# A two-layer encoder trunk with mixture of experts: weights split by whole chunks on ScalarE and VectorE, with none of it on GpSimd

## The chip, the cores and the metric

The kernel runs on one core of a Trainium2 chip. The metric is the device time of one execution in microseconds. Of the kernel before there are three runs: 1071.22 us (median), 1070.33 and 1071.66.

## The reference

The input is a residual stream x of 512 rows of 1024 floats, and 256 memory rows. Two layers follow each other. In each layer

- one projection of x feeds a token mixer (layer 0: a gated unit over chunks of 128 rows; layer 1: a short causal convolution) and the queries of a cross-attention to the memory rows; both results are concatenated, projected, added to 2^0.5 x and normalised;
- a router, shared by the layers, picks for each row one group of four experts and two experts in it; each of the 16 experts computes `silu(x @ w_gate) * (x @ w_up)` and then `@ w_down`, weighted by the router's share; the sum is added to 2^0.5 x and normalised.

```
h = jax.nn.silu(xt @ w_gate[e]) * (xt @ w_up[e])
out = out + combine[:, e:e + 1] * (h @ w_down[e])
```

w_gate and w_up are 1024 x 512 and w_down is 512 x 1024 for each expert, all float32: 6 MB an expert, 96 MB a layer. All results are float32 and are wanted close to float32 precision.

## The kernel before

**Splitting.** TensorE multiplies in the type fp32r, which keeps fewer bits than float32. So each operand is split into a high part (a copy rounded to fp32r, made on ScalarE) and a low part (what the rounding left, float32 minus high, made on VectorE, or for some weights on GpSimd). `mm3` makes a product of three matmuls: high with high, high with low, low with high.

**Pages.** SBUF is handed out in 24 pages of 8 KB a partition. `page` takes the front of a list of free pages, `drop` puts pages at its end. A page taken anew is a new tile in the same memory, and the framework lets an instruction that writes it wait for those that still use the bytes it writes.

**The stream of weights** (class `Stream`, one object `W`). All weights pass through it as chunks of 1 MB, one page each: 128 partitions x 4 x 512 floats. `fetch` takes a page, and SyncE's queue loads a chunk into it; a load also waits for the load two before it. `split` takes a page for one *half* of the oldest chunk (2 x 512 floats a partition) and puts its high part in the front half of that page and its low part in the back half; after the second half of a chunk its raw page is dropped. `next` gives the oldest half that is ready; `done` drops its page and calls `pump`. `pump` splits as long as fewer than `ahead` halves are ready, and else fetches as long as more pages are free than `keep` and what splitting still wants. All this happens while the program is written, so it fixes which page each instruction uses and the order in which the stream's work is issued; the framework's planner then sets the order on each engine from its own estimate of times.

**The experts** (`experts`). Each expert handles up to 128 rows, gathered by an indirect DMA on GpSimd's queue three experts ahead. `gate_up` takes eight halves (gate, up, gate, up, two chunks' worth of rows each), six fp32r matmuls of 512 columns for a half; then Silu on ScalarE (line 651) and the product on VectorE (line 652). `down` of the expert before takes four halves, its results are evicted on ScalarE (line 673) and added to memory by an indirect DMA. For the last expert, `down` of expert 14 stands between its two gate/up halves. That makes twelve halves, six chunks, for each expert, 96 chunks a layer. In the experts `ahead` is 4 and `keep` is 1; after expert 12 (`last - 3`) `keep` becomes 6. Three pages besides those of the stream are in use there. The halves whose running number modulo 12 is 5 or 11 have their low part made on GpSimd, as has one late half of each layer; around the routers every second one (layer 0) or two of three (layer 1).

**The other stages.** The projections use 24 matmuls for each half, with `keep` 2 to 8 and `ahead` 4 (3 or 2 around the routers).

The lines 130 (high part) and 131 (low part) are the split; lines 161 to 163 are the three matmuls of `mm3`.

Of the kernel before, what the change touches and what calls it, by code (L numbers as in the profile page):

```python
# [19 lines left out]
FR = mybir.dt.float32r  # L20
BF = mybir.dt.bfloat16
I32 = mybir.dt.int32
AF = mybir.ActivationFunctionType
# [25 lines left out]
def trunk(ctx, tc, x, mem, w_in_a, sgu_ln_g, sgu_ln_b, sgu_w, sgu_b, w_in_b, conv_w, w_kv, w_out,  # L49
# [15 lines left out]
    def page(name, shape, dtype=FT):  # L65
        assert free_pages, f"no page for {name}; held: {sorted(v[1] for v in held.values())}"
        i = free_pages.pop(0)
        uid[0] += 1
        t = pages.tile(shape, dtype, name=f"{name}_{uid[0]}", tag=f"pg{i}", bufs=1)
        held[id(t)] = (i, name, t)  # L70
        return t

    def drop(*ts):
        for t in ts:
            free_pages.append(held.pop(id(t))[0])
# [8 lines left out]
        return psum.tile([P, n], FT, name=name, tag="R", bufs=1)  # L84


    class Stream:
        def __init__(self):
            self.todo, self.raw, self.ready = [], [], []
            self.keep, self.ahead, self.stop, self.sent = 0, 4, 0, 0  # L90
            self.pooled = ()
            self.hold, self.count, self.on_pool = False, 0, lambda n: False
            self.after, self.behind, self.loads = None, None, []

        def add_pairs(self, w, k0):
# [14 lines left out]
        def fetch(self):  # L110
            self.sent += 1
            t = page("raw", [P, 4, 512])
            src = self.todo.pop(0)
            with ExitStack() if self.behind is None else tc.issue_after(self.behind):
                load = sp.dma_start(t if src.ap[-1][1] == 512 else t.rearrange("p (a b) n -> p a (b n)", a=2), src).ins
            self.loads.append(load)
            if len(self.loads) > IN_FLIGHT:
                tc.add_manual_dep(load, self.loads.pop(0).name,
                                  mybir.DependencyInfo(mybir.DependencyClass.Sync, mybir.DependencyReason.DATA),
                                  reason="few loads in flight")  # L120
            self.raw.append([t, 0])

        def split(self):
            r = self.raw[0]
            t, h = r
            g = page("split", [P, 2, 2, 512], FR)
            src = t[:, 2 * h:2 * h + 2]
            low = pool_e if self.on_pool(self.count) or self.count in self.pooled else vec
            with ExitStack() if self.after is None else tc.issue_after(self.after):
                act.activation(g[:, 0], src, AF.Copy)  # L130
            low.tensor_tensor(g[:, 1], src, g[:, 0], op=OP.subtract)  # L131
            self.count += 1
            self.ready.append(g)
            r[1] += 1
            if r[1] == 2:
                self.raw.pop(0)
                drop(t)

        def pump(self):
            while True:  # L140
                if not self.hold and len(self.ready) < self.ahead and self.raw and len(free_pages) > 0:
                    self.split()
                elif len(self.todo) > self.stop and len(free_pages) > self.keep + max(0, self.ahead - len(self.ready)):
                    self.fetch()
                else:
                    return
# [3 lines left out]
                self.pump()  # L150
            return self.ready.pop(0)

        def done(self, g):
            drop(g)
            self.pump()

    W = Stream()
# [451 lines left out]
    def experts(i, lnp, fill, after, stop, fine=False):  # L609
# [71 lines left out]
        more(i, hy)  # L681
        W.keep = 1
        W.pump()
        W.on_pool = lambda n: n % 12 in (5, 11)
        xtrans(0)
        gather(2)
        for e in range(E):
            if e == last - 1 and not fine:
                rows = page("lnrow", [2 * KB, P])
                for u, v in enumerate(lnp):  # L690
                    act.dma_start(rows[u * KB:(u + 1) * KB], v.rearrange("(k p) -> k p", p=P))
            up = gate_up(e, (lambda: (down(last - 1, scaled(last - 1)), scatter(last - 1))) if e == last else None)
            if e + 1 < E:
                xtrans(e + 1)
            if e + 3 < E:
                gather(e + 3)
            if 0 < e < last:
                down(e - 1, scaled(e - 1))
                scatter(e - 1)
            if e == last - 3:  # L700
                n = W.count + 2 * (len(W.raw) + len(W.todo) - stop) - (W.raw[0][1] if W.raw else 0)
                W.pooled = [n - k for k in (3,)]
                W.keep = 6
                W.stop = stop - 2 if stop else 0
            if e == last:
                drop(xt, xg)
                selp = page("selt", [P, 2, NC, P], FT)
                for c in range(NC):
                    vec.tensor_scalar(selp[:, 0, c, :], slot1, posp[:, c, last:last + 1], None, op0=OP.is_equal)
                t = bank([P, NC, P], "selt")  # L710
                for c in range(NC):
                    pe.transpose(t[:, c, :], selp[:, 0, c, :], ident)
                selt = page("selr", [P, NC, P], FR)
                vec.tensor_copy(selt, t)
                drop(selp)
                xs[:] = [page("x", [P, 2, D]) for _ in range(2)]
                xrow[:] = [xs[c // 2][:, c % 2, :] for c in range(NC)]
                if fine:
                    with tc.issue_after(added[last - 1].ins):
                        lnp = ln_params(*lnp, pool_e)  # L720
                for c in range(NC):
                    W.behind = sp.dma_start(xrow[c], rd[i][c * P:(c + 1) * P, :]).ins
            if e < last:
                htrans(e)
# [3 lines left out]
            act.activation(yp[:, 0, n], o, AF.Copy, scale=tabs[last][1])  # L728
            vec.scalar_tensor_tensor(yp[:, 1, n], o, tabs[last][1], yp[:, 0, n], op0=OP.mult, op1=OP.subtract)
        W.stop = 0  # L730
        W.on_pool = lambda n: False
        rs, mvs, nms = {}, {}, {}
        r = {}

# [270 lines left out]
    def mixer_end(i, ch, cl, lnp):  # L1005
        lg = [tiny(3 * E, "lg"), None]

        def after(c, normed):
            if c == 0:
                W.on_pool = (lambda n: n % 2 == 1) if i == 0 else (lambda n: n % 3 != 0)  # L1010
                W.keep, W.ahead = (2, 3) if i == 0 else (1, 2)
                W.pump()
            if c == NC - 1:
                lg[1] = bank([P, E], "lg3")
                lg.append(normed)
            logits(c, i, lg[1] if c == NC - 1 else lg[0][:, c * E:(c + 1) * E])
            if c % 2:
                drop(xs[c // 2])
            if c == 1:
                W.pump()  # L1020
        project_out(i, ch, cl, lnp, after)
        drop(lnp)
        rp = page("route", [P, 2048])
        route(0, 3, lg[0].rearrange("p (n e) -> p n e", e=E), lg[2], rp)
        route(3, 1, lg[1].rearrange("p (n e) -> p n e", e=E), lg[2], rp)
        tables()
        drop(rp)
        overflow()
        W.ahead = 4
# [91 lines left out]
```

## Time and profile before

| | |
|---|---|
| runs | 1071.22 us median (1070.33 to 1071.66) |
| the profiled execution | 1070.24 us, of which the span from the first to the last instruction is 1068.4 us |
| mean granted TensorE clock | 0.979 |
| busy: TensorE matmul, weight load | 1002.9 us (94%), 807.4 us (76%) |
| busy: VectorE, ScalarE, GpSimd | 796.7 us (75%), 658.4 us (62%), 321.5 us (30%) |
| moved by DMA | 272.30 MB, 255 GB/s in the mean |

Matmuls overlap their neighbours, so the sum of their durations is more than TensorE's busy time, and the distance from start to start is their pace. The experts of layer 0 run from about 210 to 535 us, those of layer 1 from about 730 to 1040 us. In the timelines an instruction's busy time does not include its waiting; the idle time of the engine ahead of it stands in brackets with what ended it.

### The profile page before, as it was taken

Reading aid. Unit: us, or ns where it says so; the run is one execution under the profiler, and the core shown is the slowest. Engines: PE = TensorE matmul, PEld = TensorE weight load, DVE = VectorE, ACT = ScalarE, POOL = GpSimd, SP = SyncE. Lnnn points to the kernel's source line nnn. Section 1 sums busy time; section 2 is a strip of 40 time slices with the busy share of each in tenths; the row PEclk is TensorE's granted clock in tenths of the full one; section 3 lists DMA queues with packets and bytes.
Section 4 is the critical chain, followed back from the end, with each engine's and each line's share of the span. In section 5 each row is a group of like instructions: output and inputs, shape, how many; then the busy total and the mean of one; then the engine's idle time right before and its main releaser. Section 6 shows DMA issues by size and latency. Waiting matters only on the chain.

```text
span 1068.4 us, 13339 instructions
## 1 busy us (share of the span) xinstructions
PE 1002.9 (94%) x4847; PEld 807.4 (76%) x4848; DVE 796.7 (75%) x1004; ACT 658.4 (62%) x876; POOL 321.5 (30%) x178
## 2 busy tenths in 40 slices
PE   8999999699999999899999999977999999999895
PEld 6788889587777777677678887866777777777663
DVE  4648667768888888678694565664888889887875
ACT  4536524377888888578643424234888888887762
POOL 0000014243544435233310000123444435453253
PEclk9999999999999999899999999977999999999998
DMA  9713449689999999999561423585999999999734
GB/s 322 271 40 118 156 163 322 248 287 311 308 312 334 339 325 343 327 331 342 194 235 41 158 79 121 207 336 175 320 308 344 326 341 335 329 340 328 258 61 160
DMA packets 101968, 272.30 MB, mean 255 GB/s; under 512 B 10426, under 2 KB 10966, under 8 KB 101896
## 3 DMA queue, kind: packets, MB, share of 16 engines
q1 hardware_dynamic: 89480, 242.84, 63.7%
q0 software_dynamic: 11520, 25.92, 8.9%
q10 hardware_dynamic: 896, 2.63, 0.8%
q8 instruction: 39, 0.64, 0.2%
q14 instruction: 33, 0.27, 0.1%
HBM read 261.18 MB, written 26.21 MB: 269 GB/s over the span
## 4 chain that ended last, share of the span: by engine, by line
PE 26%; DVE 11%; issue 10%; ACT 6%; DMA 3%; POOL 1%; DVEq 0%; POOLq 0%; SPq 0%; ACTq 0%
DVE split L131 7%; ACT split L130 5%; PE ya L162 2%; PE ya L163 2%; PE za L162 2%; PE za L163 2%; PE za L161 2%; PE ya L161 2%; PE oa L161 1%; PE oa L163 1%; PE oa L162 1%; PE ra L739 1%; DMA raw<-in_w_down_dram 1%; DMA raw<-in_w_gate_dram 1%; DMA rd<-y,idxs 1%
## 5 line engine op out<-in xcount | busy, mean ns | idle before, releaser
L131 DVE TENSOR_TENSOR split<-raw,split 128x1024 fp32r<-128x1024 f32 x370 | 517.0, 1422 | 119.8 <-ACT split L130 117.4
L130 ACT ACTIVATE split<-raw 128x1024 fp32r<-128x1024 f32 x444 | 457.7, 1057 | 164.3 <-DVE split L131 45.8
L131 POOL TENSOR_TENSOR split<-raw,split 128x1024 fp32r<-128x1024 f32 x74 | 181.7, 2455 | 569.9 <-ACT split L130 267.9
L162 PE MATMUL ya<-split,ht 128*128 128x512 f32 x256 | 106.0, 414 | 11.2 <-DVE split L131 11.2
L162 PE MATMUL ua<-split,xgt 128*128 128x512 f32 x256 | 105.0, 410 | 7.7 <-DVE split L131 6.5
L162 PE MATMUL ga<-split,xgt 128*128 128x512 f32 x256 | 103.8, 405 | 1.9 <-DVE split L131 1.7
L161 PE MATMUL ga<-split,xgt 128*128 128x512 f32 x256 | 103.0, 402 | 0.0
L163 PE MATMUL ya<-split,ht 128*128 128x512 f32 x256 | 101.4, 396 | 0.7 <-DVE ht L167 0.7
L161 PE MATMUL ua<-split,xgt 128*128 128x512 f32 x256 | 101.5, 397 | 0.2 <-ACT split L130 0.2
L161 PE MATMUL ya<-split,ht 128*128 128x512 f32 x256 | 101.6, 397 | 0.0
L163 PE MATMUL ua<-split,xgt 128*128 128x512 f32 x256 | 101.1, 395 | 0.0
L163 PE MATMUL ga<-split,xgt 128*128 128x512 f32 x256 | 100.6, 393 | 0.0
L162 PEld LDWEIGHTS ya<-split,ht 128*128 128x128 f32 x256 | 48.4, 189 | 31.5 <-DVE split L131 21.9
L162 PEld LDWEIGHTS ua<-split,xgt 128*128 128x128 f32 x256 | 48.8, 191 | 27.5 <-DVE split L131 15.9
L626 POOL DMA_INDIRECT xg<-x1d,idxs x32 | 53.1, 1658 | 38.9 <-PE xt L635 19.4
L161 PE MATMUL za<-xh,split 128*128 128x512 f32 x160 | 61.7, 392 | 2.0 <-ACT xh L166 2.0
L162 PE MATMUL za<-xl,split 128*128 128x512 f32 x160 | 62.5, 391 | 0.0
L162 PEld LDWEIGHTS ga<-split,xgt 128*128 128x128 f32 x256 | 48.6, 190 | 18.3 <-DVE split L131 8.8
L163 PE MATMUL za<-xh,split 128*128 128x512 f32 x160 | 61.5, 390 | 0.0
L161 PEld LDWEIGHTS ua<-split,xgt 128*128 128x128 f32 x256 | 48.8, 191 | 11.6 <-ACT split L130 0.9
L161 PEld LDWEIGHTS ya<-split,ht 128*128 128x128 f32 x256 | 48.1, 188 | 11.6 <-ACT ht L166 0.6
L161 PEld LDWEIGHTS ga<-split,xgt 128*128 128x128 f32 x256 | 49.0, 191 | 10.1 <-ACT xgt L166 0.2
(233 smaller groups left out, 1762.9 us busy)
## 6 DMA issues: line engine op xcount, KB each, us to landing
raw<-in_w_gate_dram SPq DMA_DIRECT2D x64, 1024.0 KB, 6.4
raw<-in_w_up_dram SPq DMA_DIRECT2D x64, 1024.0 KB, 5.8
raw<-in_w_down_dram SPq DMA_DIRECT2D x64, 1024.0 KB, 7.3
raw<-in_w_kv_dram SPq DMA_DIRECT2D x8, 1024.0 KB, 6.8
raw<-in_w_out_dram SPq DMA_DIRECT2D x8, 1024.0 KB, 5.1
raw<-in_w_in_b_dram SPq DMA_DIRECT2D x8, 1024.0 KB, 5.3
raw<-in_w_in_a_dram SPq DMA_DIRECT2D x6, 1024.0 KB, 5.4
x1d<-x POOLq DMA_DIRECT2D x8, 512.0 KB, 5.1
```

What stands on the lines that cost most here:

```text
L130: act.activation(g[:, 0], src, AF.Copy)
L131: low.tensor_tensor(g[:, 1], src, g[:, 0], op=OP.subtract)
L161: pe.matmul(o, a[0], b[0], start=start, stop=False)
L162: pe.matmul(o, a[0], b[1], start=False, stop=False)
L163: return pe.matmul(o, a[1], b[0], start=False, stop=stop)
L626: pool_e.indirect_dma_start(out=xg[:, e % 2], out_offset=None, in_=x1d[i], in_offset=bass.IndirectOffsetOnAxis(ap=tabs[e][0], axis=0), bou ...
L739: pe.matmul(r[c][n], ident, xrow[c][:, n * 512:(n + 1) * 512], start=True, stop=False)
```

## The change

A whole chunk is split at once: one instruction on ScalarE (2048 floats a partition) and one on VectorE, into two pages, one of high and one of low parts. `Half` shows such a pair of pages as two halves, with the indexing the matmuls had. A split takes two pages, and both come back when the second of the two halves is done. Nothing of the split is on GpSimd. `ahead` is 6 in the experts and 4 in layer 0 around the router.

```diff
+    class Half:
+        def __init__(self, high, low, at):
+            self.high, self.low, self.at = high, low, at
+        def __getitem__(self, key):
+            _, part, k, cols = key
+            return (self.low if part else self.high)[:, self.at + k, cols]
...
         def split(self):
-            r = self.raw[0]
-            t, h = r
-            g = page("split", [P, 2, 2, 512], FR)
-            src = t[:, 2 * h:2 * h + 2]
-            low = pool_e if self.on_pool(self.count) or self.count in self.pooled else vec
+            t = self.raw.pop(0)
+            g, low = page("high", [P, 4, 512], FR), page("low", [P, 4, 512], FR)
             with ExitStack() if self.after is None else tc.issue_after(self.after):
-                act.activation(g[:, 0], src, AF.Copy)
-            low.tensor_tensor(g[:, 1], src, g[:, 0], op=OP.subtract)
-            self.count += 1
-            self.ready.append(g)
-            r[1] += 1
-            if r[1] == 2:
-                self.raw.pop(0)
-                drop(t)
+                act.activation(g, t, AF.Copy)
+            vec.tensor_tensor(low, t, g, op=OP.subtract)
+            self.ready += [Half(g, low, 0), Half(g, low, 2)]
+            drop(t)
 
         def pump(self):
             while True:
-                if not self.hold and len(self.ready) < self.ahead and self.raw and len(free_pages) > 0:
+                if not self.hold and len(self.ready) + 2 <= self.ahead and self.raw and len(free_pages) > 1:
                     self.split()
-                elif len(self.todo) > self.stop and len(free_pages) > self.keep + max(0, self.ahead - len(self.ready)):
+                elif len(self.todo) > self.stop and len(free_pages) > self.keep + max(0, self.ahead - len(self.ready)) // 2 * 2:
                     self.fetch()
...
-        def done(self, g):
-            drop(g)
+        def done(self, h):
+            if h.at:
+                drop(h.high, h.low)
             self.pump()
...
         W.pump()
-        W.on_pool = lambda n: n % 12 in (5, 11)
+        W.ahead = 6
...
             if e == last - 3:
-                n = W.count + 2 * (len(W.raw) + len(W.todo) - stop) - (W.raw[0][1] if W.raw else 0)
-                W.pooled = [n - k for k in (3,)]
                 W.keep = 6
...
         W.stop = 0
-        W.on_pool = lambda n: False
+        W.ahead = 4
...
             if c == 0:
-                W.on_pool = (lambda n: n % 2 == 1) if i == 0 else (lambda n: n % 3 != 0)
-                W.keep, W.ahead = (2, 3) if i == 0 else (1, 2)
+                W.keep, W.ahead = (2, 4) if i == 0 else (1, 2)
```

## Rows read from the trace of the kernel before

**Rows 1.** ScalarE's timeline: Silu of experts 1, 12, 15 (start us, us, what).
```profile
239.10 0.58 ACT L651 ACTIVATE h<-ga 128x512 f32<-128x512 f32 x1
...
452.09 0.60 ACT L651 ACTIVATE h<-ga 128x512 f32<-128x512 f32 x1 [0.95 <-PE ga L163]
...
520.03 0.60 ACT L651 ACTIVATE h<-ga 128x512 f32<-128x512 f32 x1 [1.53 <-PE ga L163]
...
757.93 0.58 ACT L651 ACTIVATE h<-ga 128x512 f32<-128x512 f32 x1
...
965.64 0.57 ACT L651 ACTIVATE h<-ga 128x512 f32<-128x512 f32 x1
...
1033.55 0.60 ACT L651 ACTIVATE h<-ga 128x512 f32<-128x512 f32 x1 [1.29 <-PE ga L163]
```

**Rows 2.** TensorE's timeline at the start of the experts of layer 1.
```profile
735.27 0.63 PE L161 MATMUL ua<-split,xgt 128*128 128x512 f32 x1
735.69 0.63 PE L162 MATMUL ua<-split,xgt 128*128 128x512 f32 x1
...
738.03 0.40 PE L162 MATMUL ga<-split,xgt 128*128 128x512 f32 x1
738.26 0.39 PE L163 MATMUL ga<-split,xgt 128*128 128x512 f32 x1
```

**Rows 3.** The page's groups by line: TensorE, second product (last columns: idle before).
```profile
L162 PE MATMUL ya<-split,ht 128*128 128x512 f32 x256 | 106.0, 414 | 11.2 <-DVE split L131 11.2
L162 PE MATMUL ua<-split,xgt 128*128 128x512 f32 x256 | 105.0, 410 | 7.7 <-DVE split L131 6.5
L162 PE MATMUL ga<-split,xgt 128*128 128x512 f32 x256 | 103.8, 405 | 1.9 <-DVE split L131 1.7
```

**Rows 4.** Windows, one expert: window, length, PE, PEld, DVE, ACT, POOL busy, PEclk, DMA.
```profile
803.60:822.50 18.90, 18.50 (x85) 14.64 (x84) 16.82 (x15) 15.44 (x19) 8.64 (x4) 1.00 0.96 345
```

**Rows 5.** ScalarE's timeline in one expert of layer 1.
```profile
784.71 2.01 ACT L130 ACTIVATE split<-raw 128x1024 fp32r<-128x1024 f32 x2 [0.68 <-PE ya L163]
...
789.43 1.06 ACT L130 ACTIVATE split<-raw 128x1024 fp32r<-128x1024 f32 x1 [0.39 <-DVE split L131]
...
792.24 1.06 ACT L130 ACTIVATE split<-raw 128x1024 fp32r<-128x1024 f32 x1 [0.32 <-DVE split L131]
```

**Rows 6.** VectorE's timeline in the same expert.
```profile
786.75 2.58 DVE L131 TENSOR_TENSOR split<-raw,split 128x1024 fp32r<-128x1024 f32 x1 [1.47 <-ACT split L130]
...
789.86 4.70 DVE L131 TENSOR_TENSOR split<-raw,split 128x1024 fp32r<-128x1024 f32 x4
...
800.01 1.21 DVE L131 TENSOR_TENSOR split<-raw,split 128x1024 fp32r<-128x1024 f32 x1
```

**Rows 7.** Groups by line and shape over the whole span (busy us, mean ns).
```profile
L130 ACT ACTIVATE split<-raw 128x1024 fp32r<-128x1024 f32 x444 | 457.7, 1057 | 164.3 <-DVE split L131 45.8 <-PE za L163 26.0 <-PE oa L163 24.7
L131 DVE TENSOR_TENSOR split<-raw,split 128x1024 fp32r<-128x1024 f32 x370 | 517.0, 1422 | 119.8 <-ACT split L130 117.4 <-DMA raw<-in_w_gate_dram 0.7 <-DMA raw<-in_w_up_dram 0.3
L131 POOL TENSOR_TENSOR split<-raw,split 128x1024 fp32r<-128x1024 f32 x74 | 181.7, 2455 | 569.9 <-ACT split L130 267.9 <-DVE sto L433 264.5 <-DMA raw<-in_w_up_dram 21.2
...
L167 DVE TENSOR_TENSOR xgt<-xt,xgt 128x512 fp32r<-128x512 f32 x64 | 43.4, 680 | 10.1 <-ACT xgt L166 10.1
...
L166 ACT ACTIVATE xgt<-xt 128x512 fp32r<-128x512 f32 x64 | 37.2, 583 | 10.6 <-PE ua L162 8.1 <-PE xt L635 2.2
```

**Rows 8.** ScalarE's timeline at the kernel's start: the first four halves.
```profile
9.25 4.08 ACT L130 ACTIVATE split<-raw 128x1024 fp32r<-128x1024 f32 x4
```

**Rows 9.** GpSimd's timeline in the expert of rows 5 and 6.
```profile
785.85 2.41 POOL L131 TENSOR_TENSOR split<-raw,split 128x1024 fp32r<-128x1024 f32 x1 [7.46 <-ACT split L130]
```

**Rows 10.** Windows of 4 us around the routers, columns as in rows 4.
```profile
188.00:192.00 4.00, 2.83 (x31) 2.63 (x30) 3.79 (x21) 1.03 (x1) 0.00 (x0) 1.00 0.34 105
192.00:196.00 4.00, 2.47 (x21) 2.32 (x20) 3.96 (x18) 2.43 (x6) 0.75 (x1) 1.00 0.91 337
...
716.00:720.00 4.00, 0.41 (x9) 0.32 (x9) 4.00 (x23) 1.62 (x2) 0.00 (x0) 0.50 1.04 402
```

More of the change, by code (lines that the diff above doesn't have):

```diff
@@ L90, in __init__ @@
             self.keep, self.ahead, self.stop, self.sent = 0, 4, 0, 0
-            self.pooled = ()
-            self.hold, self.count, self.on_pool = False, 0, lambda n: False
+            self.hold = False
             self.after, self.behind, self.loads = None, None, []
@@ L120, in fetch @@
                                   reason="few loads in flight")
-            self.raw.append([t, 0])
+            self.raw.append(t)
         def split(self):
-            r = self.raw[0]
-            t, h = r
-            g = page("split", [P, 2, 2, 512], FR)
-            src = t[:, 2 * h:2 * h + 2]
-            low = pool_e if self.on_pool(self.count) or self.count in self.pooled else vec
-            with ExitStack() if self.after is None else tc.issue_after(self.after):
-                act.activation(g[:, 0], src, AF.Copy)
-            low.tensor_tensor(g[:, 1], src, g[:, 0], op=OP.subtract)
-            self.count += 1
-            self.ready.append(g)
-            r[1] += 1
-            if r[1] == 2:
-                self.raw.pop(0)
-                drop(t)
+            t = self.raw.pop(0)
+            g, low = page("high", [P, 4, 512], FR), page("low", [P, 4, 512], FR)
+            with ExitStack() if self.after is None else tc.issue_after(self.after):
+                act.activation(g, t, AF.Copy)
+            vec.tensor_tensor(low, t, g, op=OP.subtract)
+            self.ready += [Half(g, low, 0), Half(g, low, 2)]
+            drop(t)
         def pump(self):
             while True:
-                if not self.hold and len(self.ready) < self.ahead and self.raw and len(free_pages) > 0:
+                if not self.hold and len(self.ready) + 2 <= self.ahead and self.raw and len(free_pages) > 1:
                     self.split()
-                elif len(self.todo) > self.stop and len(free_pages) > self.keep + max(0, self.ahead - len(self.ready)):
+                elif len(self.todo) > self.stop and len(free_pages) > self.keep + max(0, self.ahead - len(self.ready)) // 2 * 2:
                     self.fetch()
```

## The prediction

> **What bounds the kernel now.** I read the page's busy table first (PE is busy 94% of the span), then the groups by line, then the engines' timelines over one steady expert, and last the start times of the Silu of each expert, which give the pace.
>
> From the third expert of a layer on, an expert takes 18.88 us: in the second layer the Silu moves from 757.93 to 965.64 in eleven experts [rows 1]. An expert eats six 1 MB chunks (two of w_gate, two of w_up, two of w_down), twelve halves, so a chunk takes 207.71 / 66 = 3.147 us. A 512-column matmul follows the last after 0.23 us at the full clock (738.03 to 738.26 [rows 2]); a chunk has 12 of them, 2.75 us, and the 12 transposes of an expert add some 0.23 us a chunk, so TensorE alone would need about 2.98 us. The rest, 0.17 us a chunk or 1 us an expert, is TensorE waiting for the low part of a split. Over the whole run those waits are 11.2 + 7.7 + 1.9 = 20.8 us of its idle time, all but a microsecond and a half put down to VectorE's subtraction [rows 3]. The DMA engines are close behind: share 0.96 and 345 GB/s in an expert [rows 4]. So TensorE, VectorE (16.82 us busy of 18.90) and DMA lie within a tenth of each other, and what the split costs decides.
>
> **What the split waits for.** This is the step on which I build. Free pages are a queue: taken from the front, put back at the end. In the experts keep is 1, so after each step one page is free.
> Before, per chunk: a half that is done returns page d1, and the first half's split takes the one page that lay free. The next done returns d2; the second half's split takes d1, its raw page t goes to the end of the queue, the fetch takes d2, and t is what stays free. So the first half of the next chunk is always split into the raw page of the chunk before. ScalarE writes only the front half of that page, whose last reader is the subtraction of the *first* half of the chunk before. The trace shows just that wait: ScalarE's split at 789.43 waited for the subtraction that began at 786.75 and ended at 789.33, and the split at 792.24 for the first of the four from 789.86 on that belongs to it, ended by 792.21 [rows 5, 6]. With halves this costs little, since ScalarE and VectorE have another half to work on meanwhile.
>
> **The change, part by part.**
> *Whole chunks.* Now two pages come back together, every second done, and the walk is: free [z]; done returns high m and low m: [z, hm, lm]. The split takes z for its high page and hm for its low page, returns the raw page t: [lm, t]. The fetch takes lm: [t]. So again the next high page is the raw page just split, but now ScalarE writes the whole of it, and its last reader is the whole subtraction of the chunk before. That subtraction waits for its own ScalarE instruction. ScalarE and VectorE therefore take turns: high(n+1) cannot start before low(n) has ended, nor low(n+1) before high(n+1). Having six halves ready does not help, as it shifts the same rate by a chunk.
>
> *The price of a turn.* No 2048-wide split is in the trace, so by the nearest rows: ScalarE takes 1057 ns for 1024 columns and 583 ns for 512 [rows 7]; doubling by the difference gives 1057 + 2 x 474 = 2.0 us, and four back to back took 4.08 us [rows 8], 1.02 each, so 1.06 + 1.02 = 2.08 is an upper end. The lower end is 1.90 (two in 2.01 us [rows 5], less one start, 583 - 474 = 109 ns; the 512 read PSUM, the others SBUF). I take 1.95. VectorE alone takes 1.21 us for 1024 [rows 6] and 0.68 for 512 [rows 7]: 1.21 + 2 x 0.53 = 2.27; ends 2.2 (two of the four in 4.70 us [rows 6], less a start of 0.15) and 2.42 (twice 1.21). I take 2.28. From a subtraction's end to the waiting ScalarE start 0.10 us pass (789.33 to 789.43), the other way about 0.04. Sum: 1.95 + 2.28 + 0.14 = 4.37 us, ends 4.2 and 4.7, against 2.98 that TensorE needs. In the wait, ScalarE holds back what is queued behind it: the evictions of ya, Silu and the high parts of xgt and ht, for which TensorE's banks wait. ScalarE stands idle 2.4 us of each turn and VectorE 2.1, and these others need some 0.6 and 0.45 us a chunk, so most fit; I add 0.03: 4.40.
> The Trainium skill (ScalarE: Activation LUTs, What ACT_TABLE_LOAD costs) gives 186 ns and 0.833 ns a column for an activation with immediate scale; by that the ScalarE turn would be 1.89 us, and the estimate for the whole kernel some 9 us lower than mine. The trace's 1057 ns at 1024 columns lies 18 ns above that formula.
>
> *How long it lasts.* A layer's experts have 96 chunks, 0 to 95. When chunk 0 is done, two chunks are split at once; the fifth (chunk 4) is the first whose high page is the raw page of the one before. With keep = 6, set after expert 12 (76 chunks), fetches pause, pages gather, and from chunk 80 on the high page is older. So chunks 4 to 79 come in turns. Silu of expert 1 is the end of chunk 6, of expert 12 chunk 72, of expert 15 chunk 92.
> Expert 1 to 12, 66 chunks: 66 x 4.40 = 290.4 us, before 207.7 (second layer) and 452.09 - 239.10 = 213.0 (first) [rows 1]: +82.7 and +77.4.
> Chunks 4 to 6: 2 x (4.40 - 3.15) = +2.5 in each.
> Expert 12 to 15, 20 chunks: 7 x 4.40 + 13 x 3.0 = 69.8, before 1033.55 - 965.64 = 67.9 and 520.03 - 452.09 = 67.9: +1.9 in each. The DMA waits which made that stretch slow before (3.4 us a chunk instead of 3.15) go: at the slower pace a chunk is wanted every 4.40 us, 238 GB/s against 345 reached.
> Together +87.1 + 81.8 = +169 us.
>
> *Nothing on GpSimd.* 74 subtractions of 2455 ns leave it [rows 7]; they lie beside everything. VectorE gets them, 222 x 2.28 = 506 us where it had 517.0: less, because a subtraction that meets one of GpSimd's (785.85 to 788.26 [rows 9]) takes 2.58 instead of 1.21 us [rows 6]. That would be worth up to the 20.8 us above, if the turns were not there; with them it is worth nothing.
> *Six ahead.* It takes two pages from the stock of raw chunks (16 to 14): nothing, as DMA is no longer short.
> *Outside the experts* keep is 2 or more, or a chunk has 24 matmuls a half and lasts 11 us: no turns that show. The first chunk of all is split in 4.3 us where the first half took 1.06 + 1.22: +1.9 (0 to 2). Around each router, subtractions of 2.28 us may stand before VectorE's short routing steps, and GpSimd takes none: -1 to +4.6 a layer, I take +1. Sum +4.
>
> The sum: 1070.24 us of the profiled execution, which is 0.98 below the median of the runs, + 169 + 4 = **1243 us**.
>
> **The rivals.**
> *No turns, and GpSimd's lock gone* (faster). If two pages were free whenever a chunk is split, or ScalarE's write did not wait for the reader of the raw page, VectorE would have 506 us of splits in short, undisturbed pieces, and the waits of TensorE for them would go: 1070.2 - 20.8 = 1049 us; not lower, for DMA is at 0.96 already and the stock of raw pages would be eaten sooner. It decides at a free queue of two pages at rest instead of one. For it: VectorE's 2.58 us next to a GpSimd split. Against it: the waits at 789.43 and 792.24, which come from the same queue. The Trainium skill (SBUF — State Buffer, Who interferes with whom) says that a VectorE instruction with two SBUF inputs and a GpSimd one that reads SBUF block each other in full; the 2.58 us agree, and by that rule alone this change would be a gain. Chance 0.09.
> *The clock falls as well* (slower still). With turns TensorE works 2.98 of 4.40 us, 68%. At 188 to 196 us it was busy 2.83 and 2.47 of 4 us and the granted clock stayed at 1.00; at 716 to 720, busy 0.41 of 4, it was 0.50 [rows 10]. At that level matmuls follow each other at 0.42 us (735.27 to 735.69 [rows 2]), a chunk takes 5.3 us and TensorE would be the bound until the clock returns. If every second chunk met it: (4.40 + 5.3) / 2 = 4.85, +0.45 x 150 = +68: 1311 us. The Trainium skill (TensorE: Matmul & The Clock Gate, What's actually happening) says the gate follows how busy the engine has lately been; no stretch of this trace has this pattern of gaps. Chance 0.07.
> *Turns that overlap in part*: should the planner or the page order let every second chunk escape, the pace would be (4.40 + 3.0) / 2 = 3.7 and the time 1070 + 150 x 0.55 + 4 = 1157. Nothing in the walk above gives such an order. Chance 0.04.
>
> **How the numbers follow.** Forecast 0.80. Its own range comes from the ends of a turn: 4.2 gives 1243 - 150 x 0.2 = 1213 and 4.7 gives 1288; with the outer terms 1205 to 1293. For 8 in 10 I widen it a little towards both rivals: 1195 to 1300. A measurement of this kernel tells about 0.2% from no change. Faster by more than that: 0.09, within: 0.02, slower: 0.89.
>
> **What would show it.** In the profile after: ScalarE's split and VectorE's split at about 1.95 and 2.28 us, alternating without overlap; each waiting mostly for the other (ScalarE some 2 us a chunk for VectorE, where it was 0.3 now and then); Silu 26.4 us apart from expert 2 to 12 in both layers, and about 18 after; TensorE's idle time nearly all before matmuls that read a split; DMA share in the experts near 0.7. Wrong if Silu comes every 18 to 19 us, if ScalarE starts a split while VectorE still works on the last one, or if the granted clock in the experts is below 0.95.

## The result, and the profile after

The changed kernel takes 1251.42 us (median of 4 runs, 1249.85 to 1253.93) against 1070.78 us (4 runs, 1069.75 to 1071.66): a ratio of 1.1674, interval 1.164 to 1.1708. The forecast was 1243, range 1195 to 1300. The profiled execution took 1253.93 us, its span is 1252.1.

The page's groups by line (busy us, mean ns of one, then the idle time before them and what ended it) answer to [rows 3, 7]:
```profile
L137 DVE TENSOR_TENSOR low<-raw,high 128x2048 fp32r<-128x2048 f32 x222 | 507.0, 2290 | 322.1 <-ACT high L136 296.8
L136 ACT ACTIVATE high<-raw 128x2048 fp32r<-128x2048 f32 x222 | 423.8, 1917 | 272.1 <-DVE low L137 165.1
...
L165 PE MATMUL ga<-low,xgt 128*128 128x512 f32 x256 | 106.6, 416 | 62.6 <-DVE low L137 62.6
L165 PE MATMUL ua<-low,xgt 128*128 128x512 f32 x256 | 106.1, 415 | 60.0 <-DVE low L137 60.0
L165 PE MATMUL ya<-low,ht 128*128 128x512 f32 x256 | 105.9, 414 | 32.2 <-DVE low L137 32.2
```
The two engines now wait for each other: VectorE 296.8 us for ScalarE's high parts, ScalarE 165.1 us for VectorE's low parts. TensorE's idle time before products that read a low part grew from 20.8 us to 62.6 + 60.0 + 32.2 = 154.8.

ScalarE's timeline in an expert of the second layer (start us, us; in brackets the idle time before and what ended it) shows the wait on every chunk, where [rows 5] had 0.3 to 0.4 us now and then:
```profile
851.70 1.92 ACT L136 ACTIVATE high<-raw 128x2048 fp32r<-128x2048 f32 x1 [0.39 <-DVE low L137]
854.34 0.60 ACT L169 ACTIVATE xgt<-xt 128x512 fp32r<-128x512 f32 x1 [0.72 <-PE ua L165]
855.97 1.92 ACT L136 ACTIVATE high<-raw 128x2048 fp32r<-128x2048 f32 x1 [1.03 <-DVE low L137]
858.84 0.60 ACT L654 ACTIVATE h<-ga 128x512 f32<-128x512 f32 x1 [0.95 <-PE ga L166]
860.25 1.92 ACT L136 ACTIVATE high<-raw 128x2048 fp32r<-128x2048 f32 x1 [0.81 <-DVE low L137]
```
VectorE's timeline beside it:
```profile
853.65 2.29 DVE L137 TENSOR_TENSOR low<-raw,high 128x2048 fp32r<-128x2048 f32 x1 [1.38 <-ACT high L136]
855.86 0.68 DVE L170 TENSOR_TENSOR xgt<-xt,xgt 128x512 fp32r<-128x512 f32 x1
857.92 2.29 DVE L137 TENSOR_TENSOR low<-raw,high 128x2048 fp32r<-128x2048 f32 x1 [1.38 <-ACT high L136]
862.20 2.29 DVE L137 TENSOR_TENSOR low<-raw,high 128x2048 fp32r<-128x2048 f32 x1 [1.99 <-ACT high L136]
```
High from 851.70 to 853.62, low from 853.65 to 855.94, high from 855.97, low from 857.92: no overlap, and gaps of 0.03 us. From one high part to the next it is 855.97 - 851.70 = 4.27 us, then 4.28. TensorE takes a low part as soon as it is there; in five chunks of six it has stood idle for 1.2 to 1.3 us by then (its timeline):
```profile
855.99 0.50 PE L165 MATMUL ga<-low,xgt 128*128 128x512 f32 x1 [1.24 <-DVE low L137]
...
860.27 0.50 PE L165 MATMUL ua<-low,xgt 128*128 128x512 f32 x1 [1.24 <-DVE low L137]
```
One expert's window (columns as in rows 4) answers to [rows 4]:
```profile
868.80:894.50 25.70, 19.51 (x85) 14.47 (x84) 16.16 (x10) 15.16 (x12) 2.61 (x2) 1.00 0.80 260
```
The expert lasts 25.7 us instead of 18.9. The same 85 records of TensorE keep it busy for 19.51 us, 76%, at a granted clock of 1.00. ScalarE and VectorE have 15.16 + 16.16 = 31.3 us of work, more than the expert lasts, though the splits of the two don't overlap: what overlaps is the other work, which fits into the pauses.

The Silu of experts 1, 12 and 15 of both layers answer to [rows 1]:
```profile
258.79 0.60 ACT L654 ACTIVATE h<-ga 128x512 f32<-128x512 f32 x1 [0.95 <-PE ga L166]
...
540.93 0.60 ACT L654 ACTIVATE h<-ga 128x512 f32<-128x512 f32 x1 [0.93 <-PE ga L166]
...
607.17 0.60 ACT L654 ACTIVATE h<-ga 128x512 f32<-128x512 f32 x1 [0.65 <-PE ga L166]
...
858.84 0.60 ACT L654 ACTIVATE h<-ga 128x512 f32<-128x512 f32 x1 [0.95 <-PE ga L166]
...
1141.03 0.60 ACT L654 ACTIVATE h<-ga 128x512 f32<-128x512 f32 x1 [0.94 <-PE ga L166]
...
1203.97 0.60 ACT L654 ACTIVATE h<-ga 128x512 f32<-128x512 f32 x1 [2.78 <-PE ga L166]
```
They cut the span into stretches, and the difference of the two spans into terms:

| stretch | before | after | difference | predicted |
|---|---|---|---|---|
| start to Silu 1, first layer | 239.1 | 258.8 | +19.7 | +5.4 |
| Silu 1 to 12, first layer | 213.0 | 282.1 | +69.1 | +77.4 |
| Silu 12 to 15, first layer | 67.9 | 66.2 | -1.7 | +1.9 |
| Silu 15 to Silu 1 of the second layer | 237.9 | 251.7 | +13.8 | +3.5 |
| Silu 1 to 12, second layer | 207.7 | 282.2 | +74.5 | +82.7 |
| Silu 12 to 15, second layer | 67.9 | 62.9 | -5.0 | +1.9 |
| Silu 15 to the end | 34.9 | 48.1 | +13.3 | 0 |
| sum | 1068.4 | 1252.1 | +183.7 | +173 |

The borders at Silu 15 don't cut off the same work in the two kernels; the section on the prediction comes back to that.

### The profile page after: what moved, and what is told of

Same layout as the page of the kernel before. It is cut to its first block, busy times and chain, and to the rows that moved or that the text cites. A ratio compares the mean times of both kernels' runs of the same rounds, so it can differ in the third digit from the quotient of the medians.

```text
span 1252.1 us, 12774 instructions
## 1 busy us (share of the span) xinstructions
PE 1040.7 (83%) x4847; PEld 812.6 (65%) x4848; DVE 780.9 (62%) x856; ACT 641.1 (51%) x654; POOL 124.0 (10%) x104
## 4 chain that ended last, share of the span: by engine, by line
issue 27%; DVE 17%; PE 14%; ACT 12%; DMA 8%; POOL 3%; POOLq 0%; DVEq 0%; ACTq 0%; SPq 0%
DVE low L137 15%; ACT high L136 12%; DMA x1d<-x 3%; DMA rd<-h,idxs 2%; PE za L164 2%; PE za L165 2%; PE za L166 2%; POOL rd L625 1%; POOL xg L629 1%; DMA rd<-y,idxs 1%; PE oa L164 1%; PE oa L165 1%; PE ra L740 1%; PE oa L166 1%; DMA raw<-in_w_up_dram 1%
## 5 line engine op out<-in xcount | busy, mean ns | idle before, releaser
L137 DVE TENSOR_TENSOR low<-raw,high 128x2048 fp32r<-128x2048 f32 x222 | 507.0, 2290 | 322.1 <-ACT high L136 296.8
L136 ACT ACTIVATE high<-raw 128x2048 fp32r<-128x2048 f32 x222 | 423.8, 1917 | 272.1 <-DVE low L137 165.1
L165 PE MATMUL ga<-low,xgt 128*128 128x512 f32 x256 | 106.6, 416 | 62.6 <-DVE low L137 62.6
L165 PE MATMUL ua<-low,xgt 128*128 128x512 f32 x256 | 106.1, 415 | 60.0 <-DVE low L137 60.0
L165 PE MATMUL ya<-low,ht 128*128 128x512 f32 x256 | 105.9, 414 | 32.2 <-DVE low L137 32.2
L165 PEld LDWEIGHTS ga<-low,xgt 128*128 128x128 f32 x256 | 48.4, 189 | 94.0 <-DVE low L137 85.4
L164 PE MATMUL ya<-high,ht 128*128 128x512 f32 x256 | 103.3, 403 | 0.0
L164 PE MATMUL ga<-high,xgt 128*128 128x512 f32 x256 | 101.4, 396 | 0.4 <-ACT xgt L169 0.3
L164 PE MATMUL ua<-high,xgt 128*128 128x512 f32 x256 | 101.3, 396 | 0.0
L166 PE MATMUL ya<-high,ht 128*128 128x512 f32 x256 | 100.9, 395 | 0.0
L166 PE MATMUL ga<-high,xgt 128*128 128x512 f32 x256 | 100.7, 394 | 0.0
L166 PE MATMUL ua<-high,xgt 128*128 128x512 f32 x256 | 100.3, 392 | 0.0
L164 PE MATMUL za<-xh,high 128*128 128x512 f32 x160 | 63.0, 400 | 2.4 <-ACT v L978 2.4
L165 PE MATMUL za<-xl,high 128*128 128x512 f32 x160 | 63.2, 395 | 0.0
L169 ACT ACTIVATE xgt<-xt 128x512 fp32r<-128x512 f32 x64 | 38.0, 597 | 38.0 <-PE ua L165 36.3
L164 PEld LDWEIGHTS ua<-high,xgt 128*128 128x128 f32 x256 | 48.4, 189 | 10.8
```

Source lines behind the costliest of these rows:

```text
L136: act.activation(g, t, AF.Copy)
L137: vec.tensor_tensor(low, t, g, op=OP.subtract)
L164: pe.matmul(o, a[0], b[0], start=start, stop=False)
L165: pe.matmul(o, a[0], b[1], start=False, stop=False)
L166: return pe.matmul(o, a[1], b[0], start=False, stop=stop)
L169: r = act.activation(hi, src, AF.Copy)
```

## The experiments

The theory is the prediction's: the split takes its high page first, gets the page that has been the raw page of the chunk before, and so ScalarE waits for the VectorE subtraction that still reads it. What follows takes away that wait in two ways, takes the parts of the change one by one, and last follows a gain that showed up on the way. All ratios are against the kernel before, which took 1071.13 to 1072.49 us beside them.

**The pages in the other order.** One line of the changed kernel:
```diff
-            g, low = page("high", [P, 4, 512], FR), page("low", [P, 4, 512], FR)
+            low, g = page("low", [P, 4, 512], FR), page("high", [P, 4, 512], FR)
```


> The changed kernel with one line turned round: the low page is taken first and the high page second. Nothing else differs: same widths, same engines, same number of pages, six halves ahead. Theory of turns (the high part is written into the raw page that VectorE is still reading): now VectorE's own low part goes into that page, and ScalarE writes a page that TensorE gave back, so ScalarE need not wait for the last subtraction. Silu of experts 2 to 12 then comes every 18 to 19 us instead of 25.66, and the time is about 1100 us (1085 to 1115): 1251 less 2 x 11 x 7.2 = 158, plus some 8 us of DMA waits that come back at the ends of the layers. Rival (wide instructions on two engines are too slow in themselves, or too late because two pages come back at once): nothing changes, 25.66 and 1250 us.

It took 1061.7 us, ratio 0.9898 (0.9869 to 0.9927): 190 us less than the changed kernel, for two names in another order. The low part now goes into the old raw page, whose last reader is VectorE itself, which is done with it when it gets there. ScalarE's timeline and VectorE's show the splits side by side, and two neighbouring Silu:
```profile
322.90 1.91 ACT L136 ACTIVATE high<-raw 128x2048 fp32r<-128x2048 f32 x1
...
326.95 0.57 ACT L654 ACTIVATE h<-ga 128x512 f32<-128x512 f32 x1
...
344.88 0.57 ACT L654 ACTIVATE h<-ga 128x512 f32<-128x512 f32 x1
```
```profile
321.86 2.29 DVE L137 TENSOR_TENSOR low<-raw,high 128x2048 fp32r<-128x2048 f32 x1 [1.50 <-ACT high L136]
```
ScalarE starts at 322.90, while VectorE works until 324.15, and an expert takes 17.93 us. The view of waits (us in total, times, longest) has the wait, 165.1 us in 150 times before the swap, nearly gone:
```profile
ACT high L136 <- DVE low L137: 7.7, 5, 2.8
```
The whole instructions (1915 and 2290 ns in the mean) are as long as they were, so the turns, and not they, are most of what the change costs. The time is below what I expected, and the lengthening at the ends of the layers went too: Silu 15 of the first layer to Silu 0 of the second is 228.3 us (226.05 before the change, 239.2 with it), and Silu 15 to the end 36.3 (34.9 and 48.1); how much of that is a border between two stretches that moved is said further down.

**Two pages free at rest.** The other way to the same end:
```diff
-        W.keep = 1
+        W.keep = 2
```


> The changed kernel with keep = 2 instead of 1 in the experts: one page more lies free, at the cost of one raw chunk of stock. Theory of turns: with two pages in the queue at rest the high part no longer goes into the raw page just read, so the turns end as in the run with the swapped pages: Silu every 18 to 19 us, 1085 to 1115 us, within 1% of that run. Rival (wide instructions in themselves): 25.66 us and 1250. If the stock of raw chunks were what counts: slower than the changed kernel or equal.

1077.86 us, ratio 1.0063 (1.0037 to 1.0089): below the range expected, and 1.5% above the swapped pages, not within 1%. Silu come 17.8 to 17.9 us apart up to expert 7 of the first layer and up to expert 9 of the second, so the turns are gone here too; later they are 18.7 to 21.5 us apart. That a stock of raw chunks that is one shorter has run out there is argued, not shown.

**Two instructions for each engine and chunk, same pages.**
```diff
-                act.activation(g, t, AF.Copy)
-            vec.tensor_tensor(low, t, g, op=OP.subtract)
+                for m in (slice(0, 2), slice(2, 4)):
+                    act.activation(g[:, m], t[:, m], AF.Copy)
+            for m in (slice(0, 2), slice(2, 4)):
+                vec.tensor_tensor(low[:, m], t[:, m], g[:, m], op=OP.subtract)
```


> The changed kernel with each chunk split by two instructions of 1024 columns on ScalarE and two on VectorE; pages and their order as in the changed kernel. Theory of turns: a write waits only for the readers of the same bytes, so the first half of the next high part waits for the first subtraction of the last chunk only; ScalarE and VectorE overlap again, a chunk costs VectorE 2 x 1.21 = 2.4 us and TensorE's 2.98 decides: Silu every 18 to 19 us, 1080 to 1110 us. Outside the experts shorter instructions also stand less in the way: of the 41 us lost there against the kernel before, 5 to 15 come back. Rival (a write waits for the whole old tile): the turn stays at 1.06 + 1.06 + 1.21 + 1.21 = 4.5 us or a little less, Silu every 26 to 27 us, 1250 to 1270 us.

1137.81 us, ratio 1.0609 (1.0564 to 1.0655), Silu 21.52 us apart: neither number. ScalarE's timeline and VectorE's (x2 is the two instructions of one chunk):
```profile
890.37 2.01 ACT L137 ACTIVATE high<-raw 128x1024 fp32r<-128x1024 f32 x2 [0.73 <-DVE low L139]
893.85 2.01 ACT L137 ACTIVATE high<-raw 128x1024 fp32r<-128x1024 f32 x2 [0.41 <-DVE low L139]
```
```profile
891.46 2.36 DVE L139 TENSOR_TENSOR low<-raw,high 128x1024 fp32r<-128x1024 f32 x2 [1.12 <-ACT high L137]
894.94 2.36 DVE L139 TENSOR_TENSOR low<-raw,high 128x1024 fp32r<-128x1024 f32 x2 [0.53 <-issue]
```
VectorE starts after ScalarE's first half (890.37 to 891.46), but ScalarE starts the next chunk only when both subtractions have ended (893.82, start 893.85). In the program only the first of each pair on ScalarE carries the wait for VectorE. So the first write to a page waits for all readers of what the page held before, not only for those of the bytes it writes, as the section on pages has it; a turn is 1.09 + 2.36 + 0.03 = 3.48 us here, and 21.52 / 6 = 3.59 in the mean, with other work that comes between. This corrects the prediction's reading of [rows 5, 6]: the wait at 789.43 was not for the first half alone. There the order written for ScalarE puts the second half of a chunk ahead of the first, and the first waits for the whole page before it; that order is what made it cheap. At the start of the kernel the shorter instructions give 7 of the 19 us back (Silu 0 of the first layer at 238.93).

**Four halves ahead, as before.**
```diff
-        W.ahead = 6
```


> The changed kernel with four halves ahead in the experts instead of six. Theory of turns: the rate is set by the turn and not by how far ahead it runs: Silu stays at 25.6 to 25.7 us, and the time within 1% of 1251. Rival (six ahead hides part of the latency of a split, 1.92 + 2.29 us): Silu later than 26.5 us, over 1270 us. A second question: the last scatter of the last layer came late behind a row of splits on VectorE; if the six ahead make that row, 5 to 13 us come back at the two layer ends.

1254.66 us, ratio 1.1718 (1.1669 to 1.1766), Silu 25.66 us apart, the ends of the layers as in the changed kernel. With the turns, six ahead is worth nothing. Then the same line taken out where the pages are swapped too:
```diff
-            g, low = page("high", [P, 4, 512], FR), page("low", [P, 4, 512], FR)
+            low, g = page("low", [P, 4, 512], FR), page("high", [P, 4, 512], FR)
...
-        W.ahead = 6
```


> The swapped pages with four halves ahead instead of six. Without the turns the lead may count: two chunks ahead cover 2 x 2.98 = 6.0 us, less the chunk in work, against 1.92 + 2.29 = 4.2 us for a split. Theory (with two chunks the next split starts only when one chunk of 2.98 us is left, so 1.2 us are missing in each): experts over 20 us, time 1100 to 1150 us. Rival (VectorE and ScalarE overlap enough): within 1% of 1062 us.

1174.76 us, ratio 1.0959 (1.0911 to 1.1007), Silu some 22 to 24.4 us apart: 113 us more than with six ahead, and above the range expected. The view of waits names the places (us in total, times, longest):
```profile
ACT xgt L169 <- PE ua L165: 119.8, 48, 4.2
...
PE ua L165 <- DVE low L137: 62.5, 37, 1.8
```
TensorE waits for a low part, and ScalarE, before it splits on, for TensorE's product ahead of xgt (36.3 us in the changed kernel). A whole chunk is split only when two halves have room, and with four ahead that comes late; that this is the cause is argued, the size is measured.

**The kernel before, without GpSimd.** Halves, and every subtraction on VectorE:
```diff
-            low = pool_e if self.on_pool(self.count) or self.count in self.pooled else vec
+            low = vec
```


> The kernel before, with halves and four ahead, and no split on GpSimd anywhere: that part of the change by itself. Theory (GpSimd's subtraction only holds up VectorE's): the waits of 2.58 us go, an expert takes 18.0 to 18.4 us instead of 18.89, and the time is 1050 to 1062 us. Rival (VectorE needs the relief): an expert takes 19 us or more, over 1072 us. For the time lost before the first expert (first Silu at 227 us before, 246 after the change, 243 with the swapped pages): if the wide instructions lose it, the first Silu here comes at 225 to 231 us; if the missing GpSimd around the router loses it, at 235 or later.

1036.1 us (1034.71 to 1036.35), ratio 0.9661 (0.9637 to 0.9686). It beats both kernels, and by more than expected. The first Silu comes at 229.08, so the missing GpSimd is not what makes the changed kernel's start late. Two Silu of the steady stretch, 18.10 us apart where it was 18.89, and the groups by line:
```profile
330.37 0.60 ACT L651 ACTIVATE h<-ga 128x512 f32<-128x512 f32 x1 [0.30 <-PE ga L163]
...
348.47 0.60 ACT L651 ACTIVATE h<-ga 128x512 f32<-128x512 f32 x1 [0.30 <-PE ga L163]
```
```profile
L131 DVE TENSOR_TENSOR split<-raw,split 128x1024 fp32r<-128x1024 f32 x444 | 526.8, 1219 | 104.8 <-ACT split L130 103.9
...
L162 PE MATMUL ya<-split,ht 128*128 128x512 f32 x256 | 105.1, 411 | 0.9 <-DVE split L131 0.9
...
L162 PE MATMUL ua<-split,xgt 128*128 128x512 f32 x256 | 103.0, 402 | 0.8 <-DVE split L131 0.8
```
VectorE does all 444 subtractions in 526.8 us; with GpSimd doing 74 of them, its 370 took 517.0 [rows 7]. GpSimd's 181.7 us of work relieved VectorE of 9.8. TensorE's waits for low parts went from 11.2 and 7.7 us [rows 3] to 0.9 and 0.8. The page's busy table says the same of whole engines:
```profile
PE 988.5 (96%) x4847; PEld 808.3 (78%) x4848; DVE 792.8 (77%) x1078; ACT 658.1 (64%) x876; POOL 132.0 (13%) x104
```
VectorE is busy 792.8 us, with 74 instructions more than in the kernel before and less time (796.7). Windows of 100 us in the experts of layer 0 (columns as in rows 4), first the kernel before, then this one, say why the gain is larger than TensorE's idle time:
```profile
300.00:400.00 100.00, 97.98 (x451) 77.89 (x450) 88.29 (x75) 81.68 (x96) 43.94 (x21) 1.00 0.94 330
...
300.00:400.00 100.00, 100.00 (x469) 81.58 (x468) 90.57 (x89) 84.98 (x100) 21.21 (x12) 1.00 0.97 339
```
TensorE is idle for only 2% of the first window, yet the second has 4% more of its instructions, as 18.10 against 18.89 us an expert. A matmul lasts 0.39 us and the next one starts 0.23 us after it [rows 2], so the first 0.16 us of every wait don't show as idle time.

**Whole chunks in the experts alone.** Swapped pages, six ahead and no GpSimd in the experts; outside them halves with GpSimd, as before. The core of it, against the changed kernel:
```diff
+            if self.whole and h == 0:
+                low, g = page("low", [P, 4, 512], FR), page("high", [P, 4, 512], FR)
+                act.activation(g, t, AF.Copy)
+                vec.tensor_tensor(low, t, g, op=OP.subtract)
...
-        W.ahead = 6
+        W.on_pool, W.whole, W.ahead = (lambda n: False), True, 6
...
-        W.ahead = 4
+        W.on_pool, W.whole, W.ahead = (lambda n: False), False, 4
...
-                W.keep, W.ahead = (2, 4) if i == 0 else (1, 2)
+                W.on_pool = (lambda n: n % 2 == 1) if i == 0 else (lambda n: n % 3 != 0)
+                W.keep, W.ahead = (2, 3) if i == 0 else (1, 2)
```


> Whole chunks with swapped pages, six ahead and no GpSimd in the experts only; outside the experts halves, four ahead and GpSimd as in the kernel before. If the wide instructions or the missing GpSimd outside the experts lose the 16 us ahead of the first Silu: first Silu at 225 to 231 us, experts as with the swapped pages (17.92 us), time 1040 to 1053 us. Rival (the loss comes from the experts' own first chunks or from the planner's order at large): first Silu at 238 or later, time 1058 to 1066 us.

1056.24 us, ratio 0.984 (0.981 to 0.987), 3 us above what was expected. Silu 0 comes at 228.93, where the changed kernel has it at 246.33, the swapped one at 242.92 and the kernel before at 227.25: the late start is the price of whole chunks outside the experts (`ahead` of 4 instead of 3 around the first router goes with them and was not tried apart). Of these 14 us against the swapped kernel only 5 reach the end. Up to Silu 15 of the first layer nothing is lost (510.74 against 527.70); at Silu 0 of the second the lead is 13 us (743.12 against 756.02), at its Silu 15 4.5 (1024.44 against 1028.98), and 9 at the end of the two profiled executions. In the last third of each layer Silu are further apart in both kernels; why is not shown. Two of the first layer on ScalarE, 22.3 us apart instead of 17.9:
```profile
399.17 0.60 ACT L675 ACTIVATE h<-ga 128x512 f32<-128x512 f32 x1 [2.35 <-PE ga L187]
...
421.50 0.60 ACT L675 ACTIVATE h<-ga 128x512 f32<-128x512 f32 x1 [0.54 <-PE ga L187]
```
The same kernel without GpSimd outside the experts:
```diff
-            low = pool_e if self.on_pool(self.count) or self.count in self.pooled else vec
+            low = vec
```


> As the run with whole chunks in the experts only, but with no split on GpSimd outside either. If the wide instructions lose the time ahead of the first Silu: first Silu at 225 to 231 us and a time within 0.5% of that run. If the missing GpSimd loses it: first Silu at 235 us or later and 8 to 20 us more than that run.

1054.17 us, ratio 0.9857 (0.9803 to 0.9911), Silu 0 at 231.39, just above the range expected: GpSimd is worth 2.5 us at the start, and at the end nothing.

**Why whole chunks stay 18 us behind halves.** Six halves ahead and two pages at a time leave 14 raw chunks in stock instead of 16. If that is it, halves without GpSimd must lose as much when they keep two pages more:
```diff
-        W.keep = 1
+        W.keep = 3
```


> Halves with nothing on GpSimd (1036 us), with keep = 3 instead of 1 in the experts: two raw chunks less of stock, 14 instead of 16, the number that the whole-chunk kernels have. Theory of stock (TensorE eats a layer's chunks faster than DMA brings them, 6 in 18.1 us against some 335 GB/s, so the stock runs down and each chunk of it that is missing is paid at the end of a layer with 1.05 MB / 335 GB/s = 3.1 us): two chunks, two layers: +12.5 us, 1046 to 1052 us, with Silu 18.1 us apart up to expert 8 or 9 and over 20 us apart after. That would account for most of the 18 to 20 us by which whole chunks in the experts are slower than halves. Rival (the loss of whole chunks is their late splits, not the stock): 1034 to 1040 us.

1045.34 us, ratio 0.9751 (0.9705 to 0.9796), Silu 17.97 us apart up to expert 9 and then about 19.6, not over 20. Two chunks of stock cost 9 us, somewhat less than expected; if the whole chunks pay as much for theirs, that is half of the distance. The other way about, a page more of stock, in halves without GpSimd and in whole chunks in the experts alone:
```diff
-        W.keep = 1
+        W.keep = 0
```


> Halves with nothing on GpSimd and keep = 0 in the experts: one raw chunk more of stock, but a split now writes into the page that TensorE has just given back. Theory of stock: one chunk, two layers: -6 us, 1028 to 1033 us. Rival (ScalarE then waits for TensorE's last matmul with each half, 1.06 + 1.22 us before the next half is ready against three halves of 1.49 us still ahead, so little; or DMA gains nothing): 1034 to 1040 us; slower than 1040 if the wait costs more than the stock gives.

> Whole chunks with swapped pages in the experts (1056 us), with keep = 0: one raw chunk more of stock; each load goes into the raw page just split. Theory of stock: -6 us, 1047 to 1053 us. Rival (the load waits for VectorE's subtraction, the high part for TensorE's last matmul of the chunk): 1056 us or more, experts over 18.2 us from the start.

1035.53 us, ratio 0.965 (0.9607 to 0.9693) with halves, 1056.96 us, ratio 0.9846 (0.98 to 0.9892) with whole chunks in the experts: no gain in either. The other 9 to 11 us between whole chunks and halves stay open.

## Why the prediction was right, and where not

*The turns* are as foretold: ScalarE and VectorE alternate in both layers, TensorE waits for low parts, and either of two edits that take the page's last reader away, without shortening an instruction, gives 174 to 190 us back. The detail of the wait was misread (same columns only; it is the whole old page). For the change it made no difference, as one instruction wrote the whole page anyway. ScalarE waits 1.1 us at a time for VectorE (165.1 us in 150 times), not the 2 us foretold; the rest of its pause in a turn is spent on waits for TensorE by the work between.

*The price of a turn* was 4.40 us, measured 25.66 / 6 = 4.28: ScalarE 1.92 (forecast 1.95), VectorE 2.29 (2.28), the two gaps 0.06 (0.14), and nothing for the work between (0.03). 66 turns in each layer make 8 us of difference each, just the distance between +77.4 and +69.1, +82.7 and +74.5. The Trainium skill (ScalarE: Activation LUTs, What ACT_TABLE_LOAD costs) gives 186 ns + 0.833 ns a column, by which 2048 columns take an estimated 1.89 us; the trace's 1917 ns lies 25 ns above that, so the page was nearer than my 1.95.

*How long it lasts.* The end of the turns after expert 12 is seen (66.2 and 62.9 us for three experts, 77.0 at the pace of the turns). That these stretches came to -1.7 and -5.0 instead of +1.9 each shows no larger gain from DMA waits: the border at their end moved, as the next paragraph shows. The first turns came later than foretold, or cost less: from Silu 0 to Silu 1 each layer took 0.6 us more, not 2.5.

*Outside the experts* is the term that failed: with +4 foretold, some +46 came by the borders of the table. Of it 19 us lie ahead of the first Silu, where 2.9 were foretold. The cost that I looked for, the first chunk, is small; but all along the start the same splits stand in order with short steps. One of them, in TensorE's timeline:
```profile
46.61 1.97 PE L269 MATMUL tr<-ident,x 128*128 128x128 f32 x8 [4.91 <-DVE xl L170]
...
49.72 2.00 PE L164 MATMUL za<-xh,high 128*128 128x512 f32 x4
```
and what VectorE and ScalarE did before it:
```profile
43.66 2.29 DVE L137 TENSOR_TENSOR low<-raw,high 128x2048 fp32r<-128x2048 f32 x1 [0.99 <-ACT high L136]
45.87 1.88 DVE L170 TENSOR_TENSOR xl<-tr,xh 128x512 fp32r<-128x512 f32 x3
```
```profile
41.72 1.91 ACT L136 ACTIVATE high<-raw 128x2048 fp32r<-128x2048 f32 x1
43.52 1.57 ACT L169 ACTIVATE xh<-tr 128x512 fp32r<-128x512 f32 x3
```
The low parts of x stand behind a subtraction of 2.29 us, and their high parts behind a split of 1.91 us. TensorE's first products of za start at 49.72; in the kernel before they started 9 us earlier:
```profile
40.29 1.21 PE L161 MATMUL za<-xh,split 128*128 128x512 f32 x4 [2.00 <-ACT xh L166]
```
Whole chunks in the experts alone bring the first Silu back to 228.93.

The other 26 us lie after Silu 15, where I had put 1 us (around the second layer's router). Most of them are no loss there, but a border that moved. GpSimd's timeline has the scatter of expert 14, first in the kernel before, then in the changed one:
```profile
1032.18 2.37 POOL L622 DMA_INDIRECT rd<-h,idxs  x1
...
1214.77 1.55 POOL L625 DMA_INDIRECT rd<-h,idxs  x1 [8.91 <-ACT h L676]
```
It stood ahead of Silu 15 (1033.55) and now stands 11 us behind it (1203.97); in the first layer it is 514.99 against 520.03 and 612.80 against 607.17. In TensorE's order the gate products of expert 15 now come ahead of most products of ya for expert 14, which run up to 1213.8, where they had ended at 1029.6: Silu 15 comes earlier, and the same work is counted after it. Silu 14 is a better border. ScalarE's timeline, in the kernel before (both layers) and in the changed one:
```profile
490.73 0.60 ACT L651 ACTIVATE h<-ga 128x512 f32<-128x512 f32 x1 [2.15 <-PE ga L163]
...
1004.67 0.60 ACT L651 ACTIVATE h<-ga 128x512 f32<-128x512 f32 x1 [2.15 <-PE ga L163]
...
586.82 0.60 ACT L654 ACTIVATE h<-ga 128x512 f32<-128x512 f32 x1 [0.54 <-PE ga L166]
...
1189.47 0.59 ACT L654 ACTIVATE h<-ga 128x512 f32<-128x512 f32 x1
```
From Silu 12 to Silu 14, twelve chunks, the experts take 45.9 and 48.4 us instead of 38.6 and 39.0; the prediction's own prices give 7 x 4.40 + 5 x 3.0 = 45.8, so the end of the turns was priced about right. From Silu 14 to Silu 0 of the second layer it is +4.2 us (259.6 against 255.4), and from Silu 14 of the second layer to the end -1.1 (62.6 against 63.7). There the prediction, which let the DMA waits go (eight chunks at 3.0 us instead of 29.3 and 28.9 us, and 1 us for the router), comes to -4.3 and -4.9. So 12 us more came there than foretold; why is open. The swapped pages have +2.7 and -2.5 there, so at most a small part of it is the turns.

So the start cost 16 us more than foretold and the ends of the layers, from Silu 12 on, 15 us more; the turns from Silu 1 to 12 cost 16.5 us less and the first ones 4 less. They partly cancelled: the sum is 11 us off on the profiled span, 8 against the median, with larger errors inside. That it is so close is in part luck.

*Nothing on GpSimd, six ahead.* With the turns both were to be worth nothing; for six ahead its removal shows it, for GpSimd no run with turns has it back. Without them the bound of 20.8 us for GpSimd was too low: the kernel before gains 35 us. 24 of it are the steady stretches (213.0 and 207.7 us become 198.4 each), 11 the last three experts of both layers. The bound was taken from TensorE's idle time, which does not show the first 0.16 us of each wait. And six ahead, priced at nothing, saves whole chunks from a loss of 113 us.

*The rivals.* In the experts the granted clock stayed at 1.00 with TensorE pausing 1.2 to 1.3 us in five chunks of six, so the fall of the clock is out. Turns that overlap in part did not come; the experiment with two instructions made them, at 1138 us. The rival without turns, 1049 us, lies 13 us below what the swapped pages give, 1061.7; there the steady experts gain (17.93 us each) and the start loses 16 us. The rule behind it (the Trainium skill, SBUF — State Buffer, Who interferes with whom: a VectorE instruction with two SBUF inputs contends with a GpSimd one that reads SBUF) agrees with the 0.9661 of halves without GpSimd; in the change its gain was hidden by the turns. No run separates that contention from the length of GpSimd's own subtractions (2455 ns). The DMA share in the experts was 0.80, not near 0.7, though the traffic fell to 260 of 345 GB/s, three quarters; why the share fell by less stays open.

## What to carry to other kernels

Where free buffers are a queue, walk by hand which buffer each write gets and who reads its old content last. With one buffer free at rest that is the work of a moment ago, and if the last reader is another engine, two engines that should overlap take turns; give that buffer to the engine that read it last, or keep one more free. An elementwise operation shared out between VectorE and GpSimd is worth measuring against VectorE alone, and a kernel's width of instruction is worth choosing by stage: what is harmless in a stage of long products delays the short steps of another.

## What the runs showed of the hardware

74 subtractions of 2455 ns on GpSimd took only 9.8 us off VectorE's work, and cost the kernel 35 us. Instructions twice as wide saved little by themselves: 1.92 us for 2048 columns on ScalarE against 2.01 for two of 1024, 2.29 on VectorE against 2.36 for two. A wait of TensorE costs more than its idle time says: 2% idle went with 4% fewer instructions. TensorE kept a granted clock of 1.00 in the experts while it stood still for 6.2 us of every 25.7, in pauses of 1.2 to 1.3 us.
